# Later steps for the next expert's preparations, and three buffers for activations, in a hybrid decoder layer with 32 experts

## The chip, the cores and the metric

The kernel runs on one core of one Trainium2 chip. The metric is the time on the device, in microseconds (us), as the median of several runs; smaller is better. One further run of the same kernel was taken with the hardware profiler, and its trace is read below.

## The reference, cut to what matters

One layer of a decoder on 1024 tokens of width 1024. First a mixer (dilated attention beside a gated recurrence, one input and one output projection), then a mixture of experts. All in float32. The change lies in the second part:

```
logits = h @ w_router + b_router
top_val, top_idx = top_k(logits, 4)          # 4 of 32 experts for each token
gates = softmax(top_val)
# for each expert e, on the rows that chose it:
hg = rows @ w_gu[e] + b_gu[e]                # 1024 -> 2048
glu, lin = min(hg[:, :1024], 7), clip(hg[:, 1024:], -7, 7)
act = glu * sigmoid(1.702 * glu) * (lin + 1)
y = (act @ w_down[e] + b_down[e]) * gate     # 1024 -> 1024
out[token] += y
x = x + gate_f * RMSNorm_post(out)
```

An expert has 12.6 MB of weights, all 32 have 403 MB, and each is read once.

## The kernel before, in words

**Order of the experts.** After the mixer the experts are sorted by how many rows they got. The sorted place k fixes a capacity `CAPS[k]`: 352, 288, 256, 240, 224, 208, 200, 192, 180, 176, 164, 160, 152, 148, 144, 136 rows for k = 0 to 15, 128 for k = 16 to 29, 64 for k = 30 and 31. Three classes compute them: `Many` (over 128 rows), `Few` (128) and `Half` (64). `ORDER` alternates them: 1, 30, 0, 31, 2, 16, 3, 17, ... 15, 29. So there are 32 rounds of the loop in `moe`, each with a current expert `cur` and a next one `nxt`, and 31 of them prepare a next one.

**Pieces of weights.** A piece is 1 MB of weights: 128 partitions x 4 x 512 float32. It is loaded by the SP queue into `raw` (4 buffers), copied by ScalarE to a rounded high part `wh` (L283, 4 instructions to a piece, 4 buffers), and VectorE writes the rest into `wl` (L284, 4 instructions, 3 buffers). TensorE then multiplies with high and low parts: in `Few` 12 matmuls of 512 columns to a piece (L291, L292, L294), in `Many` 32 (for capacities up to 256: 16 of twice the capacity and 16 of the capacity, L533). An expert has four steps `gu(0)` to `gu(3)` for the first product and two steps `down(0)`, `down(1)` for the second, each of two pieces: 12 pieces.

**Preparations.** `prep()` of the next expert is a generator. Up to its first `yield` it reads the expert's number and its table of rows, issues the indirect DMA that gathers the rows into `xg` (L623, POOL queue; tag `row`, 6 buffers shared with the results `y`), and takes its tiles. The steps behind that turn `xg` on TensorE through PSUM and split it: in `Few` two steps of four transposes (L302, tile `pts`), each with a copy to `xh` on ScalarE (L304) and a subtraction to `xl` on VectorE (L305); in `Many` one step of four transposes for each half of each block of 128 rows (L508, tile `pxb`; L511 ScalarE and L512 VectorE write `xb`), and a last step that turns the bias (L515, tile `pbb`; L517). In `Half` there is one step (L432). The transposes share two PSUM buffers (tag `tp`).

**Activations.** In `Few`, `gu(c)` ends with `swiglu`, whose last instruction writes `act` (L330). A generator `finish` then turns `act` (L302 again, two transposes) and splits it to `ah`, `al`. `Half` has a `finish` too. In `Many` with a capacity of up to 180, or over 256, `down` has a `finish` that turns the results back (L590, tile `pyb`), one step for each block of 128 rows.

**The side queue.** `Side` holds such generators in the order in which they were added, each with a due time. `add` runs the generator to its first `yield` at once. Each piece of weights ends with a call `side()`: it counts one up and takes up to two steps of the generator at the head, if its due time has passed. A generator behind the head is not looked at. With `wait=1` the first steps come at the second call behind `add`. `until(steps)` runs everything down to that generator. The order of tracing is the priority by which a scheduler orders each engine's instructions when the program is built, and each engine runs its own list in order.

One round: `prep()` of the next expert is added, then come `gu(1)`, `gu(2)`, `gu(3)` of the current one, then `until(prep)`, `gu(0)` of the next one, `until(last)`, `down(0)` and `down(1)` of the current one. So the calls of `side()` in a round are: two in each of `gu(1)`, `gu(2)`, `gu(3)`, the next `gu(0)`, `down(0)`, `down(1)`.

Of the kernel before, what the change touches and what calls it, by code (L numbers as in the profile page):

```python
# [121 lines left out]
def moe_biases(g, tc, wp, wk):  # L122
    nc = tc.nc
    bg = wp.tile([128, 2 * FF], F32, name="bgraw", tag="raw")
    nc.gpsimd.memset(bg[64:128], 0.0)
    for s in range(2):
        ld = nc.sync.dma_start(bg[32 * s:32 * s + 32], g.b_gu[0])
        tc.add_manual_dep(ld.ins, g.gathered.name, SYNC, reason="the first rows come first")
    g.bg = wk.tile([128, 2 * FF], F32R, name="bgsplit", tag="bgs", bufs=1)
    nc.scalar.activation(g.bg, bg, AF.Copy)  # L130
    nc.vector.tensor_sub(g.bg[32:64], bg[32:64], g.bg[32:64].bitcast(F32))


def down_biases(g, tc, wk):

    nc = tc.nc
    raw = wk.tile([96, D], F32, name="bdraw", tag="pwl")
    for s in range(3):
        nc.scalar.dma_start(raw[32 * s:32 * s + 32], g.b_down[0])
    g.bd = wk.tile([96, D], F32R, name="bd", tag="wada")  # L140
    nc.vector.tensor_copy(g.bd, raw)
    nc.vector.tensor_sub(g.bd[64:96], raw[64:96], g.bd[64:96].bitcast(F32))
# [525 lines left out]
def moe(g, tc, wp, wk, sm, ps):  # L668
    g.pieces, g.gathered, g.asked = 0, None, None
    todo = [(Many if CAPS[k] > 128 else Few if CAPS[k] > 64 else Half)(g, tc, k, (wp, wk, sm, ps)) for k in ORDER]  # L670
    side = Side()
    cur = todo[0]
    prep = cur.prep()
    side.add(prep)
    side.until(prep)
    side.add(cur.gu(0, side))
    moe_biases(g, tc, wp, wk)
    overflow_lists(g, tc, sm, ps)
    for nxt in todo[1:] + [None]:
        if nxt:  # L680
            prep = nxt.prep()
            side.add(prep)
        side.add(cur.gu(1, side))
        side.add(cur.gu(2, side))
        last = cur.gu(3, side)
        side.add(last)
        if nxt:
            side.until(prep)
            side.add(nxt.gu(0, side))
        side.until(last)  # L690
        side.add(cur.down(0, side))
        last = cur.down(1, side)
        side.add(last)
        if nxt:
            cur = nxt
    side.until(last)
    g.last_y = cur.y[0]
# [80 lines left out]
def ada(g, tc, cst, wk, sm, ps, dram):  # L778
    nc = tc.nc
    cr = wk.tile([8, 128], F32, name="cr", tag="oo")  # L780
    nc.sync.dma_start(cr, g.c.rearrange("o (k p) -> (o k) p", p=128))
    cs = wk.tile([8, 128], F32, name="cs", tag="oo")
    nc.scalar.activation(cs, cr, AF.Sigmoid)
    nc.vector.tensor_mul(cs, cs, cr)
    pt = ps.tile([128, 512], F32, name="pct", tag="tp")
    nc.tensor.transpose(pt[:, :8], cs, g.ident[:8, :8])
    g.cT = cst.tile([128, 8], F32, name="cT")
    nc.vector.tensor_copy(g.cT, pt[:, :8])
    g.onec = cst.tile([128, 1], F32, name="onec")
    nc.vector.memset(g.onec, 1.0)  # L790
    g.mod_d = dram.tile([6, D], F32, name="mod_d")
# [151 lines left out]
def vec_cols(g, tc, cst, wk, sm, ps):  # L943
    nc = tc.nc
    rows = wk.tile([24, 128], F32, name="vrows", tag="oo")
    nc.sync.dma_start(rows[0:8], g.g_pre_mix.rearrange("o (k p) -> (o k) p", p=128))
    nc.sync.dma_start(rows[8:12], g.attn_norm_w.rearrange("o (k p) -> (o k) p", p=128))
    nc.sync.dma_start(rows[12:16], g.hgrn_norm_w.rearrange("o (k p) -> (o k) p", p=128))
    nc.sync.dma_start(rows[16:24], g.hgrn_lb.rearrange("o (k p) -> (o k) p", p=128))
    pt = ps.tile([128, 512], F32, name="pvt", tag="tp")  # L950
    nc.tensor.transpose(pt[:, :24], rows, g.ident[:24, :24])
    v = cst.tile([128, 24], F32, name="vcols")
    nc.vector.tensor_copy(v, pt[:, :24])
    g.gpre, g.anw, g.hnw = v[:, 0:8], v[:, 8:12], v[:, 12:16]
    m = sm.tile([128, 4], F32, name="lbm")
    nc.vector.tensor_max(m, v[:, 16:20], v[:, 20:24])
    e = sm.tile([128, 2, 4], F32, name="lbe")
    for s in range(2):
        nc.vector.tensor_sub(e[:, s], v[:, 16 + 4 * s:20 + 4 * s], m)
    nc.scalar.activation(e, e, AF.Exp)  # L960
    nc.vector.tensor_add(m, e[:, 0], e[:, 1])
    nc.vector.reciprocal(m, m)
    g.lb = cst.tile([128, 4], F32, name="lb")
    g.lb1 = cst.tile([128, 4], F32, name="lb1")
    nc.vector.tensor_mul(g.lb, e[:, 0], m)
    nc.vector.tensor_scalar(g.lb1, g.lb, -1.0, 1.0, op0=OP.mult, op1=OP.add)
# [49 lines left out]
def hgrn_consts(g, tc, cst, wk):  # L1016
    nc = tc.nc
    d = wk.tile([128, 128], F32, name="hdist", tag="vt")
    nc.gpsimd.iota(d, pattern=[[1, 128]], base=0, channel_multiplier=-1, allow_small_or_imprecise_dtypes=True)
    nc.vector.tensor_scalar(d, d, 0.0, None, op0=OP.is_ge)  # L1020
    g.hmask = cst.tile([128, 128], mybir.dt.uint8, name="hmask")
    nc.vector.tensor_copy(g.hmask, d)
    g.at = []
    for i in range(2):
        z = cst.tile([128, 128], F32, name=f"at{i}")
        nc.vector.memset(z, 0.0)
        g.at.append(z)
# [566 lines left out]
@with_exitstack  # L1594
def layer(ctx: ExitStack, tc: tile.TileContext, args):
    g = Ctx()
    for n, a in args.items():
        setattr(g, n, a)
    cst = ctx.enter_context(tc.tile_pool(name="cst", bufs=1))
    g.cst = cst  # L1600
    dram = ctx.enter_context(tc.tile_pool(name="dram", bufs=1, space=DRAM))
    with ExitStack() as mx:
        ps = Pool(mx.enter_context(tc.tile_pool(name="ps", bufs=1, space=PSUM)),
                  {"mm": 2, "s": 2, "tp": 2, "o": 1, "pa": 1})
        big = mx.enter_context(tc.tile_pool(name="big", bufs=1))
        yp = mx.enter_context(tc.tile_pool(name="yp", bufs=1))
        wk = Pool(mx.enter_context(tc.tile_pool(name="wk", bufs=1)),
                  {"pj": 5, "w": 3, "vt": 1, "pt": 2, "wraw": 2, "wada": 1, "acc": 1, "oo": 2, "kk": 1, "pwh": 2, "pwl": 2, "hf": 1})
        cm = mx.enter_context(tc.tile_pool(name="cm", bufs=1))
        sm = mx.enter_context(tc.tile_pool(name="sm", bufs=1))  # L1610
        consts(g, tc, cst, cm, wk)
        ada(g, tc, cm, wk, sm, ps, dram)
        vec_cols(g, tc, cm, wk, sm, ps)
        g.y = [yp.tile([128, T], F32, name=f"y{k}") for k in range(KT)]

        def masks():
            hgrn_consts(g, tc, cm, wk)
            attn_bias(g, tc, cm, wk)

        make_h(g, tc, cm, big, wk, sm, ps, masks)  # L1620
        g.side = chain(*(ada_group(g, tc, q, wk, sm, ps) for q in (1, 2)))
        mixer(g, tc, wk, sm, ps, lambda: moe_setup(g, tc, cm, wk, dram))
        wout_split(g, tc, big, wk)
        bcast_rows(g, tc, wk)
        down_biases(g, tc, wk)
        router_consts(g, tc, cm, wk, sm, ps)
        rows = [mix_out_tile(g, tc, t, wk, sm, ps) for t in range(NT)]
        for t in range(NT + 1):
            if t:
                next(rows[t - 1])  # L1630
            if t < NT:
                next(rows[t])
            if t and t < NT - 1:
                next(rows[t])
            if t:
                next(rows[t - 1])
            if t in (0, NT - 1):
                next(rows[t])
            if 1 < t < NT:
                next(rows[t - 2], None)  # L1640
            if t >= NT - 1:
                next(rows[t - 1], None)
        sort_experts(g, tc, cst, sm, ps)
    ps = Pool(ctx.enter_context(tc.tile_pool(name="ps2", bufs=1, space=PSUM)), {"mm": 3, "tp": 2})
    wp = Pool(ctx.enter_context(tc.tile_pool(name="wp", bufs=1)), {"raw": 4, "wh": 4, "wl": 3})
    wk = Pool(ctx.enter_context(tc.tile_pool(name="wk2", bufs=1)),
              {"row": 6, "xh": 1, "xl": 1, "ah": 1, "al": 1, "xb": 1, "ab": 1, "gl": 2, "sg": 1,
               "gm": 1, "sga": 1, "lc": 1, "act": 1})
    sm = ctx.enter_context(tc.tile_pool(name="sm2", bufs=1))
    moe(g, tc, wp, wk, sm, ps)  # L1650
    final_load(g, tc, wk, sm)
    overflow(g, tc, wp, wk, sm, ps)
    final(g, tc, wp, wk, sm)
# [22 lines left out]
```

## Time and profile before

| what | value |
| --- | --- |
| median of 3 runs | 2327.73 us (2326.22 to 2332.06) |
| the profiled run | 2331.19 us |
| its span, first to last instruction | 2329.6 us |
| TensorE busy with matmuls | 2204.8 us (95%) |
| VectorE, ScalarE, GpSimd busy | 1762.8 us (76%), 1437.5 us (62%), 275.4 us (12%) |
| moved by DMA | 530.24 MB, mean 228 GB/s |
| mean granted TensorE clock | 0.975 |

The mixer takes about the first 710 us, the experts run from there to about 2290 us, and what is left is the last norm and the sum. Times in the rows below are in us from the start of the span, durations of single instructions in ns where marked. "PEclk" is the granted TensorE clock as a share of the full one: 1.00 is 2.4 GHz, 0.50 is 1.2 GHz.

### The profile page before, as it was taken

Reading aid. Unit: us, or ns where it says so; the run is one execution under the profiler, and the core shown is the slowest. Engines: PE = TensorE matmul, PEld = TensorE weight load, DVE = VectorE, ACT = ScalarE, POOL = GpSimd, SP = SyncE. Lnnn points to the kernel's source line nnn. Section 1 sums busy time; section 2 is a strip of 40 time slices with the busy share of each in tenths; the row PEclk is TensorE's granted clock in tenths of the full one; section 3 lists DMA queues with packets and bytes.
Section 4 is the critical chain, followed back from the end, with each engine's and each line's share of the span. In section 5 each row is a group of like instructions: output and inputs, shape, how many; then the busy total and the mean of one; then the engine's idle time right before and its main releaser. Section 6 shows DMA issues by size and latency. Waiting matters only on the chain. (4 is left out here: it accounts for less than half of the span.)

```text
span 2329.6 us, 38808 instructions
## 1 busy us (share of the span) xinstructions
PE 2204.8 (95%) x13342; PEld 1867.8 (80%) x13342; DVE 1762.8 (76%) x3887; ACT 1437.5 (62%) x3092; POOL 275.4 (12%) x239
## 2 busy tenths in 40 slices
PE   6999999998986999999999999999999999999992
PEld 3766667886766999788798888979899899899891
DVE  5466647556776675778797887979889899988985
ACT  6343442324545675767676776767777777777773
POOL 2000000000233020211011111101111111111000
PEclk8999999998997999999999999999999999999996
DMA  6333201113348695979798988989989999999997
GB/s 256 118 100 100 83 19 49 39 46 114 113 151 247 213 284 175 292 221 304 246 310 267 287 285 269 318 262 310 300 287 318 311 306 318 307 314 313 309 314 228
DMA packets 399937, 530.24 MB, mean 228 GB/s; under 512 B 17284, under 2 KB 308412, under 8 KB 398648
## 3 DMA queue, kind: packets, MB, share of 16 engines
q1 hardware_dynamic: 382736, 477.18, 61.6%
q0 software_dynamic: 15664, 45.92, 8.6%
q10 hardware_dynamic: 1336, 4.63, 0.5%
q8 instruction: 106, 1.74, 0.3%
q14 instruction: 95, 0.78, 0.1%
HBM read 487.91 MB, written 39.75 MB: 227 GB/s over the span
## 5 line engine op out<-in xcount | busy, mean ns | idle before, releaser
L284 DVE TENSOR_TENSOR wl<-raw,wh 128x512 fp32r<-128x512 f32 x1536 | 976.3, 686 | 153.1 <-ACT wh L283 60.5
L283 ACT ACTIVATE wh<-raw 128x512 fp32r<-128x512 f32 x1536 | 852.4, 623 | 240.4 <-DMA raw<-in_w_down_dram 61.1
L533 PE MATMUL pgb<-xb,wh 128*128 128x288 f32 (+13 forms) x2304 | 473.1, 333 | 3.2 <-DVE gl L553 2.8
L533 PEld LDWEIGHTS pgb<-xb,wh 128*128 128x128 f32 x2304 | 360.5, 190 | 11.9 <-DVE gl L553 3.5
L533 PE MATMUL pgb<-xb,wl 128*128 128x288 f32 (+15 forms) x2048 | 301.3, 274 | 0.0
L533 PEld LDWEIGHTS pgb<-xb,wl 128*128 128x128 f32 x2048 | 290.6, 190 | 5.3
L632 POOL DMA_INDIRECT yacc<-y,tab x52 | 111.3, 2141 | 1033.2 <-ACT y L373 487.7
L291 PE MATMUL pg<-wh,xh 128*128 128x512 f32 x448 | 180.3, 402 | 0.0
L292 PE MATMUL pg<-wh,xl 128*128 128x512 f32 x448 | 175.2, 391 | 0.0
L533 PE MATMUL pdb<-ab,wh 128*128 128x288 f32 (+7 forms) x768 | 142.5, 314 | 0.0
L551 ACT ACTIVATE gl<-pgb,bcol 128x288 f32<-128x288 f32 (+15 forms) x256 | 94.1, 421 | 75.5 <-PE pgb L533 75.2
L995 PE MATMUL pp<-hh,pwh 128*128 128x512 f32 x448 | 130.6, 411 | 7.5 <-DVE y L1055 4.4
L995 PE MATMUL pp<-hl,pwh 128*128 128x512 f32 x448 | 130.8, 408 | 0.9 <-DVE hl L932 0.9
L995 PE MATMUL pp<-hh,pwl 128*128 128x512 f32 x448 | 129.2, 406 | 0.0
L294 PE MATMUL pg<-wl,xh 128*128 128x512 f32 x448 | 120.1, 390 | 0.0
L533 PEld LDWEIGHTS pdb<-ab,wh 128*128 128x128 f32 x768 | 115.1, 189 | 1.1 <-DVE yt L581 0.2
L995 PEld LDWEIGHTS pp<-hh,pwh 128*128 128x128 f32 x448 | 82.3, 193 | 26.1 <-DVE y L1055 4.8
L294 PEld LDWEIGHTS pg<-wl,xh 128*128 128x128 f32 x448 | 84.1, 188 | 18.0
L291 PEld LDWEIGHTS pg<-wh,xh 128*128 128x128 f32 x448 | 84.2, 188 | 16.8
L995 PEld LDWEIGHTS pp<-hh,pwl 128*128 128x128 f32 x448 | 81.6, 190 | 19.7 <-issue 5.4
L292 PEld LDWEIGHTS pg<-wh,xl 128*128 128x128 f32 x448 | 84.3, 188 | 15.8
L369 PE MATMUL pd<-wh,ab 128*128 128x512 f32 (+5 forms) x384 | 96.8, 394 | 0.0
(447 smaller groups left out, 3416.2 us busy)
## 6 DMA issues: line engine op xcount, KB each, us to landing
raw<-in_w_gu_dram SPq DMA_DIRECT2D x512, 512.0 KB
raw<-in_w_down_dram SPq DMA_DIRECT2D x128, 1024.0 KB
wada<-in_w_ada_dram SPq DMA_DIRECT2D x32, 512.0 KB
wraw<-in_w_in_dram SPq DMA_DIRECT2D x28, 512.0 KB
wada<-in_w_ada_dram SPq DMA_DIRECT2D x8, 1024.0 KB
x<-in_x_dram SPq DMA_DIRECT2D x8, 512.0 KB
oraw<-in_w_out_dram SPq DMA_DIRECT2D x8, 512.0 KB
xo<-in_x_dram SPq DMA_DIRECT2D x8, 512.0 KB
```

Of the source, the lines that this page charges most:

```text
L283: nc.scalar.activation(h, r, AF.Copy)
L284: nc.vector.tensor_sub(lo, r, h.bitcast(F32))
L291: nc.tensor.matmul(out, xh[:, k0 + i, :], wh[:, i, :], start=start and i == 0, stop=False)
L292: nc.tensor.matmul(out, xl[:, k0 + i, :], wh[:, i, :], start=False, stop=False)
L294: nc.tensor.matmul(out, xh[:, k0 + i, :], wl[:, i, :], start=False, stop=stop and i == HK - 1)
L369: nc.tensor.matmul(p[j][:r], m(j, a, s * HK + i), w[:, i, :], start=s + a + i == 0 and w is wh, stop=s == 1 and w is wl and i == HK - 1)
L533: nc.tensor.matmul(o, w, x, start=s == 0 and j == 0, stop=s == 1 and j == len(seq) - 1, skip_group_check=True)
L551: nc.scalar.activation(gl[:, t, h], src, AF.Identity, bias=self.bias[:, j:j + 1])
L632: b.tc.nc.gpsimd.indirect_dma_start(out=b.g.yacc[:, :], out_offset=bass.IndirectOffsetOnAxis(ap=rows, axis=0), in_=y, in_offset=None, comp ...
L995: nc.tensor.matmul(p, a[:, kt, :], b[:, kt, hs], start=n == 0, stop=n == 3 * KT - 1)
```

## The change

A generator of preparations is now added with a wait of two calls, except in the two rounds whose current expert is of class `Half`. The tag `act` gets three buffers where it had one.

```diff
@@ moe
     for nxt in todo[1:] + [None]:
         if nxt:
             prep = nxt.prep()
-            side.add(prep)
+            side.add(prep, 1 if isinstance(cur, Half) else 2)
         side.add(cur.gu(1, side))
         side.add(cur.gu(2, side))
         last = cur.gu(3, side)
@@ layer
     wk = Pool(ctx.enter_context(tc.tile_pool(name="wk2", bufs=1)),
               {"row": 6, "xh": 1, "xl": 1, "ah": 1, "al": 1, "xb": 1, "ab": 1, "gl": 2, "sg": 1,
-               "gm": 1, "sga": 1, "lc": 1, "act": 1})
+               "gm": 1, "sga": 1, "lc": 1, "act": 3})
```

## Rows read from the trace of the kernel before

**Rows 1.** Stretches: us, then busy us of each engine, PEclk, DMA share, GB/s.
```profile
1600.00:1800.00 200.00, 200.00 (x1273) 184.81 (x1271) 177.79 (x344) 153.04 (x318) 29.65 (x21) 1.00 0.95 302
2000.00:2200.00 200.00, 198.60 (x1310) 180.28 (x1309) 179.71 (x357) 154.66 (x326) 30.23 (x22) 1.00 0.96 308
```

**Rows 2.** Waits of TensorE, 710 to 2300 us: total us, times, longest us.
```profile
PE pts L302 <- DMA xg<-hrows,tab: 5.0, 1, 5.0
PE pbb L515 <- DVE xb L512: 4.0, 5, 1.3
PE pts L302 <- DVE act L330: 4.0, 1, 4.0
PE pgb L533 <- DVE gl L553: 2.8, 5, 1.1
...
PE pts L302 <- DVE xb L512: 0.7, 3, 0.3
```

**Rows 3.** Timeline of TensorE around 988 us: start, length, what, idle before.
```profile
988.17 1.97 PE L302 MATMUL pts<-ident,xg 128*128 128x128 f32 x8 [4.95 <-DMA xg<-hrows,tab]
...
992.40 1.09 PE L533 MATMUL pgb<-xb,wh 128*128 128x512 f32 x4
...
993.81 1.09 PE L533 MATMUL pgb<-xb,wh 128*128 128x512 f32 x4
```

**Rows 4.** The stretch with the lower clock, columns as in the first group.
```profile
985.50:992.20 6.70, 4.03 (x15) 3.65 (x16) 2.44 (x5) 2.62 (x5) 1.43 (x1) 0.50 1.03 294
```

**Rows 5.** Timeline of GpSimd, the gather for expert 16.
```profile
973.74 8.50 POOL L623 DMA_INDIRECT xg<-hrows,tab  x1 [4.68 <-DMA tab<-table]
```

**Rows 6.** Timeline of VectorE in the same stretch.
```profile
972.83 8.52 DVE L284 TENSOR_TENSOR wl<-raw,wh 128x512 fp32r<-128x512 f32 x14
...
983.36 2.49 DVE L284 TENSOR_TENSOR wl<-raw,wh 128x512 fp32r<-128x512 f32 x4
```

**Rows 7.** Tile xg: all its gathers (ns min/median/max), and issue to landing.
```profile
L623 POOL DMA_INDIRECT xg<-hrows,tab x50: 920/1129/8501, 713.8 to 2193.2; - x50
...
DMA to landing us min/median/max: 5.8/6.9/8.7
```

**Rows 8.** Timeline of TensorE, second transposes and bias for expert 5.
```profile
1255.00 0.88 PE L508 MATMUL pxb<-ident,xg 128*128 128x128 f32 x8
...
1259.50 0.23 PE L515 MATMUL pbb<-ident,br 16*128 16x16 f32 x1 [0.60 <-DVE xb L512]
```

**Rows 9.** Timeline of ScalarE beside them.
```profile
1257.09 1.15 ACT L283 ACTIVATE wh<-raw 128x512 fp32r<-128x512 f32 x2 [0.80 <-DMA raw<-in_w_gu_dram]
1258.14 0.90 ACT L511 ACTIVATE xb<-pxb 128x512 fp32r<-128x512 f32 x2
```

**Rows 10.** Timeline of TensorE, the same work for expert 9.
```profile
1638.41 1.04 PE L590 MATMUL pyb<-ident,yt 128*128 128x128 f32 x8
...
1646.06 0.97 PE L508 MATMUL pxb<-ident,xg 128*128 128x128 f32 x8
...
1649.89 0.23 PE L515 MATMUL pbb<-ident,br 16*128 16x16 f32 x1
```

**Rows 11.** Timeline of ScalarE beside them.
```profile
1647.25 0.79 ACT L511 ACTIVATE xb<-pxb 128x512 fp32r<-128x512 f32 x2
```

**Rows 12.** Timelines of TensorE, ScalarE and VectorE, turning the rows of expert 17.
```profile
1094.05 1.03 PE L302 MATMUL pts<-ident,xg 128*128 128x128 f32 x8
...
1094.95 1.08 ACT L304 ACTIVATE xh<-pts 128x512 fp32r<-128x512 f32 x2
...
1095.75 1.28 DVE L305 TENSOR_TENSOR xl<-pts,xh 128x512 fp32r<-128x512 f32 x2
```

**Rows 13.** VectorE by line, 1600 to 2200 us: busy us, mean ns, idle before.
```profile
L330 DVE SCALAR_TENSOR_TENSOR act<-lc,gm 128x256 f32<-128x256 f32 x28 | 11.8, 422 | 1.9 <-PE pts L302 1.9
```

**Rows 14.** Waits of the DMA queue of the weights, 710 to 2300 us.
```profile
SPq L310 <- DVE wl L284: 566.2, 239, 8.0
SPq L316 <- DVE wl L284: 499.2, 124, 9.2
```

## The prediction

> **What bounds the kernel now.** I read the table of stretches first, then TensorE's waits, then the timelines of the engines at the longest of them. From 1600 to 1800 us TensorE is busy in all 200.00 us at a clock of 1.00, and from 2000 to 2200 in 198.60, with VectorE next at 178 to 180 and the DMA engines at a share of 0.95 [rows 1]. So with the experts an edit is worth what it takes from TensorE's waits, and no more. The DMA share looks like a second bound, but the queue that loads the weights spends 566.2 + 499.2 us of this part waiting until VectorE frees a buffer [rows 14]: the loads are held back, not late on the whole.
>
> TensorE's waits in this part are few [rows 2]. The reader is to see three that touch the change: one of 5.0 us for the gathered rows of a `Few` expert, five that make 4.0 us ahead of the transposed bias of a `Many` expert, and three that make 0.7 us ahead of the transposes right behind it. Two others matter less: 2.8 us in five for a PSUM buffer that VectorE empties, and 4.0 us for the last expert's activations.
>
> **The change part by part.** Which rounds move? By `Side`, steps added with `wait=2` come at the third call instead of the second, that is behind the first piece of `gu(2)` instead of behind `gu(1)`. Two of the 31 rounds have a `Half` as current expert and keep 1. In seven (current experts 22 to 28) the queue's head is the down `finish` of the `Many` before; it takes its two steps at the second call, and the preparations start at the third one already. That leaves 22: two preparations of `Half`, 14 of `Few`, six of `Many` (experts 3 to 8). What comes before the first `yield` (register loads, table, gather, bias load) runs in `add` and is not moved, so the POOL and SP queues keep their order. Moved are transposes on TensorE, their copies on ScalarE and subtractions on VectorE. No instruction is added.
>
> *The wait for the gather.* It is in the first preparation of a `Few`, for expert 16. TensorE stopped 4.95 us and went on at 988.17 [rows 3], so it came there at 983.22. The gather had been at work on GpSimd from 973.74 to 982.24 [rows 5] and landed 5.9 us later, near the fastest of all gathers (5.8) [rows 7]. A piece of this expert takes 5.64 us: eight matmuls go by from 992.40 to 993.81, 1.41 us [rows 3], and a piece has 32. With the transposes one piece later TensorE gets there at 983.22 + 5.64 = 988.86, 0.7 us behind the landing. The wait goes. With it goes what it cost afterwards: during the stop the granted clock fell to 0.50 (1.2 GHz) and stood there from 985.5 to 992.2, and TensorE worked 4.03 us of that [rows 4], 2.0 us more than at full clock. Together 7.0 us. What comes next there is the first tile of the second piece, which waits for nothing that the trace shows. Bounds: if the gather lands as slowly as the slowest (8.7 us), at 990.9, 2.1 us of waiting stay and the gain is 4.9; the upper end is 7.0. I take 7.0. The other 13 `Few` preparations show no such wait and gain nothing here.
>
> Why did that gather take 8.50 us on GpSimd, where the median is 1.129 us [rows 5, 7]? Beside it VectorE ran 14 subtractions without a break, 972.83 to 981.35, and the gather was through 0.9 us after the last [rows 6].
>
> The Trainium skill, "SBUF — State Buffer", section "SBUF: two separate sides", says that VectorE and GpSimd share one pair of ports as an exclusive lock, and that a DMA issued by GpSimd can't write its descriptors while VectorE holds it. By that rule the landing hangs on where VectorE's run breaks off, not on the gather's place in its queue; this trace agrees, with the 0.9 us above. As the run lies ahead of the moved steps, the rule leaves the sum as it is, but it makes a rival, below.
>
> *The waits at the bias.* The bias goes into the PSUM buffer of the third `pxb`, so it waits for VectorE's `xb` of that one. For expert 5, TensorE turned the second pair at 1255.00 to 1255.88, but ScalarE's copies began at 1258.14, since weight splits stood ahead of them in its list, and these waited for their load (0.80 us) [rows 8, 9]. The seven rounds that already run in the new order are a natural test: for expert 9 the second pair began at 1646.06, ScalarE's copies came at 1647.25, and the bias at 1649.89 waited for nothing [rows 10, 11]; none of the seven has such a wait, all five lie before 1600 us. But they differ in one thing: 16 transposes back (`pyb`, 1.04 us for eight [rows 10]) stretch the round and give the weights time. Bounds: all 4.0 + 0.7 = 4.7 us go; or, as the steps come nearer to the pieces that wait for their loads, each of six rounds waits the longest seen, 1.3 us, which is 7.8 - 4.7 = 3.1 us worse. The seven rounds are nearest. I take two thirds of the gain, 3.0 us.
>
> *The moved copies of `Few`.* Two copies (1.08 us) and two subtractions (1.28 us) [rows 12] now come inside `gu(2)` and no longer beside the emptying of `gu(1)`'s PSUM. Cover: ScalarE and VectorE run some pieces ahead of TensorE. Bounds: the five PSUM waits (2.8 us [rows 2]) go, or the 1.28 us come on the path in each of 14 rounds, 17.9 us. I take 0: VectorE has some 20 us idle in 200 [rows 1], and the work is the same.
>
> *Three buffers.* With the moved order the activation of `gu(1)` is turned behind the writing of that of `gu(2)`. In the seven rounds that did so with one buffer, VectorE waited 1.9 us in all [rows 13], and TensorE not at all. So the buffers gain 0, and they avoid that wait in six rounds more. The rows `xg` stay one piece longer, up to 5.64 us here; gathers run tens of us ahead of their transposes but for expert 16, so that costs 0.
>
> Sum: 7.0 + 3.0 = 10.0 us. Of the profiled run: 2331.19 - 10.0 = 2321.2; what lies outside the span (1.6 us) stays. The median of the runs shown is 3.46 us below the profiled one, so I forecast 2327.73 - 10.0 = 2317.7 us.
>
> **The rivals.**
> 1. Only the gather's wait goes, and ScalarE's list holds the second pair back as before. For it: the load that held it back is still there. Against: the seven rounds. 2327.7 - 7.0 = 2320.7.
> 2. The gather slips. Two `Half` preparations upstream move as well, and VectorE's run before 981 us may come without its break, on through the four subtractions that end at 985.85 [rows 6]. Then the gather is through at 986.7 and lands at 992.6, 3.7 us behind TensorE, which costs that and up to 2.0 for the clock: of 10.0 some 4.3 stay, or 1.3 without the bias. About 2325. Against: the margin is small, but nothing moved lies between 972 and 983. The page named above is what makes it thinkable.
> 3. The order on TensorE hardly changes, since a scheduler has the last word. Against: each block of the trace follows the traced order, but for a few by the first experts. 2327.7.
> 4. Slower: the moved copies stand in VectorE's list ahead of the splits that TensorE needs next, and each of the 14 `Few` preparations delays it by 1.28 us: 2327.7 - 10.0 + 17.9 = 2335.6. For it: VectorE is busy 0.89 of the time, and TensorE did wait for its emptying five times. It decides from 10.0 / 14 = 0.7 us a round. Against: with the same copies beside the emptying itself these waits make only 2.8 us in all.
>
> **How the numbers follow.** Chances: forecast 0.50, rival 1 0.20, rival 2 0.14, rival 3 0.05, rival 4 0.11. A measurement here can tell about 0.3%, 7.0 us, from no change, so the lines are 2320.7 and 2334.7. Of the forecast 0.44 is faster and 0.06 (gather or bias worth less) within; rival 1 lies on the line, 0.10 each; rivals 2 and 3 are within, 0.19; rival 4 is slower by 0.10 and within by 0.01. Faster 0.54, same 0.36, slower 0.10. Range: the best case is 7.0 + 4.7 + 2.8 = 14.5 us, 2313.2; upwards it has to hold rivals 2 and 3 and the noise of a median, 2328.5. Outside are rival 4 and some 0.06 below.
>
> **What would show it.** Right: in TensorE's waits the row for `xg` is gone or under 1 us, the clock is 1.00 around 988, the transposes of expert 16 stand 32 matmuls later, and the bias waits sum to under 2 us. Wrong: a wait for `xg` of 2 us or more, wherever it stands; bias waits of 4 us or more; or new waits for `wl` or PSUM that sum to over 5 us from 1000 to 2275 us.

## The result, and the profile after

Over 10 runs each, the changed kernel takes 2339.43 us (median; 2334.67 to 2347.94) and the kernel before 2326.36 us (2321.1 to 2332.06). The ratio is 1.0063 with a 95% interval of 1.0049 to 1.0077: slower by some 13 us. The forecast was 2317.7 us, a range of 2313.0 to 2328.5, and a chance of 0.10 for slower.

The two profiled runs lie closer together, 2331.19 and 2335.55 us, since the first was one of the slower runs of its kernel and the second one of the faster. The page of the changed kernel, its span and TensorE's busy time:

```profile
span 2333.9 us, 38806 instructions
...
PE 2204.9 (94%) x13342; PEld 1868.0 (80%) x13342; DVE 1761.3 (75%) x3887; ACT 1437.7 (62%) x3092; POOL 260.8 (11%) x239
```

TensorE's busy time is the same to 0.1 us (2204.8 before), so what this profile loses against the first shows as waiting. TensorE's waits in the part with the experts, columns as in [rows 2]:

```profile
PE pgb L533 <- DVE gl L553: 7.0, 6, 2.0
PE pxb L508 <- DVE xb L512: 6.0, 6, 1.3
PE pts L302 <- DVE act L330: 4.5, 2, 2.9
PE pbb L515 <- DVE xb L512: 1.8, 5, 0.5
PE pdb L533 <- DVE yt L581: 1.0, 1, 1.0
...
PE pts L302 <- DVE xb L512: 0.7, 3, 0.3
```

Against [rows 2] the row for `xg` is gone (5.0 us) and the bias waits fell from 4.0 to 1.8. But there is a new row of 6.0 us in six, ahead of the second pair of transposes `pxb`, and the waits for a PSUM buffer rose from 2.8 to 7.0.

**The gather.** The gather on GpSimd, and the transposes of expert 16, which answer to [rows 5] and [rows 3]:

```profile
968.33 1.21 POOL L623 DMA_INDIRECT xg<-hrows,tab  x1 [4.59 <-DMA tab<-table]
```

```profile
985.85 1.04 PE L302 MATMUL pts<-ident,xg 128*128 128x128 f32 x8
```

Nothing waits there, and the clock stayed at 1.00. But this gather took 1.21 us on GpSimd, not 8.50, so it would not have been late in its old place either.

**The second pair.** TensorE and ScalarE in the round of expert 16, which prepares expert 3:

```profile
1039.67 0.98 PE L508 MATMUL pxb<-ident,xg 128*128 128x128 f32 x8
...
1044.82 1.13 PE L508 MATMUL pxb<-ident,xg 128*128 128x128 f32 x8 [1.15 <-DVE xb L512]
...
1049.02 0.23 PE L515 MATMUL pbb<-ident,br 16*128 16x16 f32 x1 [0.31 <-DVE xb L512]
```

```profile
1040.99 0.63 ACT L283 ACTIVATE wh<-raw 128x512 fp32r<-128x512 f32 x1 [2.51 <-DMA raw<-in_w_gu_dram]
1042.41 1.15 ACT L283 ACTIVATE wh<-raw 128x512 fp32r<-128x512 f32 x2 [0.78 <-DMA raw<-in_w_gu_dram]
1043.46 1.01 ACT L511 ACTIVATE xb<-pxb 128x512 fp32r<-128x512 f32 x2
```

The first pair was turned by 1040.65, but ScalarE's copies of it came at 1043.46. Three splits stood ahead of them in its list, and ScalarE sat idle for 2.51 and 0.78 us until their weights had landed. The second pair needs the first one's PSUM buffers, so TensorE stood. In the kernel before, the same three splits stood behind these copies and ahead of the second pair's, as [rows 8, 9] show it for expert 5, and it was the bias that waited.

**The PSUM waits.** Around 2139 us, in the round that prepares expert 28, TensorE, ScalarE and VectorE:

```profile
2130.33 1.05 PE L302 MATMUL pts<-ident,xg 128*128 128x128 f32 x8
...
2138.95 0.79 PE L533 MATMUL pgb<-xb,wh 128*128 128x288 f32 x4 [1.78 <-DVE gl L553]
```

```profile
2133.85 1.67 ACT L283 ACTIVATE wh<-raw 128x512 fp32r<-128x512 f32 x3 [2.04 <-DMA raw<-in_w_gu_dram]
2135.43 1.07 ACT L304 ACTIVATE xh<-pts 128x512 fp32r<-128x512 f32 x2
2136.39 0.63 ACT L283 ACTIVATE wh<-raw 128x512 fp32r<-128x512 f32 x1
2136.91 1.20 ACT L551 ACTIVATE gl<-pgb,bcol 128x144 f32<-128x144 f32 x4
```

```profile
2136.04 1.29 DVE L305 TENSOR_TENSOR xl<-pts,xh 128x512 fp32r<-128x512 f32 x2 [2.53 <-ACT xh L304]
2137.25 1.28 DVE L284 TENSOR_TENSOR wl<-raw,wh 128x512 fp32r<-128x512 f32 x2
2138.45 0.45 DVE L553 TENSOR_TENSOR gl<-gl,pgb 128x288 f32<-128x288 f32 x1
```

The transposes were done at 2131.4. Their copies stood behind three splits that waited 2.04 us for a load, and ahead of the emptying of PSUM (`gl`) in ScalarE's list; in VectorE's list the two subtractions held up the emptying as well. TensorE got its buffer at 2138.95, 1.78 us late. Not all of this is new: in the kernel before, TensorE waited at the same place as well.

```profile
2138.92 0.79 PE L533 MATMUL pgb<-xb,wh 128*128 128x288 f32 x4 [1.02 <-DVE gl L553]
```

By these two profiles 0.76 us of this wait are new; over all rounds the row grew from 2.8 to 7.0 us. Behind the longest wait of the row, 1.99 us at 2230, the granted clock stayed at 1.00; behind this one it fell to 0.50 for 3.4 us, within this stretch:

```profile
2140.00:2144.00 4.00, 4.00 (x23) 4.00 (x21) 3.46 (x10) 1.96 (x5) 2.11 (x3) 0.57 0.93 322
```

### The profile page after: what moved, and what is told of

The parts are those of the page before. It is cut to its first block, busy times and chain, and to the rows that moved or that the text cites. A ratio compares the mean times of both kernels' runs of the same rounds, so it can differ in the third digit from the quotient of the medians.

```text
span 2333.9 us, 38806 instructions
## 1 busy us (share of the span) xinstructions
PE 2204.9 (94%) x13342; PEld 1868.0 (80%) x13342; DVE 1761.3 (75%) x3887; ACT 1437.7 (62%) x3092; POOL 260.8 (11%) x239
```

## The experiments

The first theory after the result: the change is three edits in one, the gather's wait is a gain, and the six preparations of `Many` and the 13 other ones of `Few` each lose more than that. The rival: all moved steps are harmless or good, and the gain is given back elsewhere.

**One preparation alone**, that of expert 16:

```
-            side.add(prep)
+            side.add(prep, 2 if cur.k == 2 else 1)
```

> The due time is moved for one preparation alone, that of expert 16, the first Few; act keeps one buffer. Theory (the gather's wait is a gain, and the other moved preparations lose more than that): the wait of 5.0 us for xg goes and the clock stays at 1.00 around 983 to 992, all else as before: 7 us faster than before, about 2319. Rival (the gain is given back further on, since the loads lose the head start that the stop gave them): within 3 us of before.

Measured: 2320.71 us against 2326.83, ratio 0.9971 (0.9960 to 0.9983). The theory holds. In this profile the gather was slow, and yet nothing waited:

```profile
969.24 11.15 POOL L623 DMA_INDIRECT xg<-hrows,tab  x1 [4.66 <-DMA tab<-table]
```

```profile
987.16 1.04 PE L302 MATMUL pts<-ident,xg 128*128 128x128 f32 x8
```

**The 13 other preparations of `Few` alone:**

```
-            side.add(prep)
+            side.add(prep, 2 if isinstance(cur, Many) and cur.k > 2 else 1)
```

> The due time is moved for the 13 other preparations of class Few alone; act keeps one buffer. Theory (the copies to xh and xl now stand ahead of the emptying of PSUM in the lists of ScalarE and VectorE): the wait for xg of 5.0 us stays, TensorE's waits for PSUM (pgb behind gl) rise from 2.8 to about 7 us, all of it in the last seven of these rounds, where a piece takes least time: 5 to 8 us slower, about 2333. Rival (these rounds are as good as before, and the whole loss is with the Many preparations): same within 2 us.

Measured: 2334.26 us against 2326.83, ratio 1.0037 (1.0022 to 1.0051). TensorE's waits from 1600 us on:

```profile
PE pgb L533 <- DVE gl L553: 6.9, 7, 1.9
```

As the theory said, and all seven lie behind 1860 us. The steps `gu(1)` to `gu(3)` of `Many` from 1050 us on, from the first matmul of each `gu(1)` to the first of the `Few` behind it, take 367.9 us in all, against 358.4 with the three buffers alone. That is more than the waits grew, since the clock stood at 0.50 for 10.2 us behind one of them; TensorE worked through nearly all of that, which makes some 5 us by estimate.

**The six preparations of `Many` alone:**

```
-            side.add(prep)
+            side.add(prep, 2 if type(cur) is Few else 1)
...
-               "gm": 1, "sga": 1, "lc": 1, "act": 1})
+               "gm": 1, "sga": 1, "lc": 1, "act": 3})
```

> The due time is moved for the six preparations of class Many in rounds of class Few alone, with three buffers for act. Theory (ScalarE's list has the first pair of copies behind splits that wait for their load, and the second pair of transposes waits for the first pair's buffer): a wait of 0.7 to 1.5 us ahead of the second pair (pxb) in each of the six rounds, 6 us, and 1.8 us at the bias in place of 4.0: 4 to 6 us slower, about 2332. Rival (the step as I predicted it): 3 us faster, no wait at pxb.

Measured: 2335.82 us against 2326.83, ratio 1.0044 (1.0027 to 1.0061). TensorE's waits from 1030 to 1600 us:

```profile
PE pxb L508 <- DVE xb L512: 6.9, 6, 1.8
PE pbb L515 <- DVE xb L512: 1.9, 5, 0.6
PE pts L302 <- DVE xb L512: 0.7, 3, 0.3
```

The six rounds, from the first matmul of `gu(1)` to the first of the next expert's `gu(0)`, take 129.4 us against 121.8 with the buffers alone. Of these 7.6 us the waits make 5.8 (9.5 against 3.7), and TensorE's busy time, which grew from 117.9 to 119.5 us, nearly all of the rest. The loss in time, 9.0 us, is above the 4 to 6 that I expected.

**The three buffers alone:**

```
-               "gm": 1, "sga": 1, "lc": 1, "act": 1})
+               "gm": 1, "sga": 1, "lc": 1, "act": 3})
```

> Only the three buffers for act. TensorE's, ScalarE's and the queues' lists are those of before; in seven rounds VectorE writes act one instruction earlier. Theory: its wait of 1.9 us goes, and the time is the same within 2 us, 2326. Rival (the 2 KB more move the tiles behind them in memory, and that costs in every run): 5 us slower or more, with the same waits.

Measured: 2327.82 us against 2326.83, ratio 1.0003 (0.9989 to 1.0017): nothing. Its profiled run took 2320.31 us, without a wait for `xg`, though the transposes stood in their old place. It is the better partner for the changed kernel's profile: spans of 2318.7 and 2333.9 us, both without that wait, differ by 15.2, of which the six rounds of `Few` make 6.7 and the late steps of `Many` 6.6.

**Why the second pair waits.** The splits of the next expert's first piece are ordered behind the first pair's copies, in the six rounds and in the seven later ones that prepare a `Many`, all else as with the six `Many` preparations. TensorE's list stays the same, and so do the queues'; VectorE's subtractions follow ScalarE's new order.

```
# split(..., after=()), for each high part:
hi = nc.scalar.activation(h, r, AF.Copy).ins
for x in after:
    tc.add_manual_dep(hi, x.name, NOSYNC, reason="rows first")
# piece(), for (c, s) == (0, 0) of a Many with k > 2: after = the first two xb copies of prep()
```

> As the kernel with only the Many preparations moved, but the splits of the next expert's first piece are ordered behind the first pair's two copies (xb) in ScalarE's list. TensorE's list is the same instruction by instruction. Theory (the pair's copies stood behind three splits that wait for their load): the waits ahead of the second pair of transposes (6.9 us in six) fall below 1 us, those at the bias stay at 2 to 3 us, and the time is 4 to 7 us below that kernel, about 2330. Rival (the waits come from VectorE's backlog or from the transposes' place itself): the waits stay at 5 us or more, 2336.

Measured: 2327.23 us against 2324.85, ratio 1.0013 (0.9996 to 1.0030). ScalarE in the round that prepares expert 3, and TensorE's waits from 1030 to 1600 us:

```profile
1049.17 1.03 ACT L511 ACTIVATE xb<-pxb 128x512 fp32r<-128x512 f32 x2 [1.82 <-PE pxb L508]
1050.09 0.63 ACT L283 ACTIVATE wh<-raw 128x512 fp32r<-128x512 f32 x1
1051.16 2.23 ACT L283 ACTIVATE wh<-raw 128x512 fp32r<-128x512 f32 x4 [0.44 <-DMA raw<-in_w_gu_dram]
```

```profile
PE pbb L515 <- DVE xb L512: 1.9, 3, 1.0
PE pd L369 <- DVE al L305: 0.6, 1, 0.6
PE pts L302 <- DVE xb L512: 0.5, 2, 0.3
```

The row of 6.9 us is gone, the six rounds take 120.7 us in place of 129.4, and of the 9.0 us some 2.4 are left, which the interval does not tell from none. So it was the copies' place in ScalarE's list, behind splits that wait for their load, and nothing about the transposes' place on TensorE.

**The kernel before, once more:**

> The kernel before once more, one execution. Theory (the gather for expert 16 loses a race with VectorE's run of 14 subtractions in some executions and not in others): either the gather takes 8 us or more on GpSimd and TensorE waits some 5 us for xg, or it takes under 2 us and nothing waits; the span differs by about 7 us between the two. Rival (the wait is the same in every execution): 8.5 us again and 5 us of waiting.

Measured: 2330.4 us in the one run. The gather was slow again, and TensorE waited:

```profile
970.49 9.86 POOL L623 DMA_INDIRECT xg<-hrows,tab  x1 [4.87 <-DMA tab<-table]
```

```profile
986.46 1.97 PE L302 MATMUL pts<-ident,xg 128*128 128x128 f32 x8 [4.71 <-DMA xg<-hrows,tab]
```

Alone it doesn't tell the theory from the rival; with the other profiles it does. In seven the transposes of expert 16 are in their old place. In four of these the gather took 8.50 to 11.37 us on GpSimd and TensorE waited 4.7 to 5.2; in three it took 1.02 to 1.44 and nothing waited. In the six with the new place it was slow four times (8.24 to 11.15) and nothing ever waited.

**Why the PSUM waits.** The 13 `Few` preparations by three calls:

```
-            side.add(prep)
+            side.add(prep, 3 if isinstance(cur, Many) and cur.k > 2 else 1)
```

> As the kernel with only the 13 other Few preparations moved, but by three calls: the transposes come behind the second piece of gu(2), where they stand to the emptying of gu(2) as they stood before to that of gu(1). Theory (what costs is the place of the copies ahead of an emptying of PSUM): the waits for PSUM fall back to 1 to 3 us and the time to that of before, 2327. Rival (a later place is worse in itself, since VectorE has less room there): waits of 7 us or more, 2334 or more.

Measured: 2326.02 us against 2324.85, ratio 1.0013 (0.9994 to 1.0033). ScalarE in the round that prepares expert 28, and the waits from 1600 us on:

```profile
2136.95 1.17 ACT L551 ACTIVATE gl<-pgb,bcol 128x144 f32<-128x144 f32 x4
2138.00 1.10 ACT L304 ACTIVATE xh<-pts 128x512 fp32r<-128x512 f32 x2
```

```profile
PE pdb L533 <- DVE yt L581: 2.3, 2, 1.6
PE pgb L533 <- DVE gl L553: 2.1, 3, 1.1
```

The copies stand behind the emptying, and the waits for PSUM are back at 2.1 us. A later place is not worse in itself: two calls cost 7 us, three cost nothing that can be told. Whether it is ScalarE's list or VectorE's that costs the 7 us, these runs do not separate. A wait of 2.3 us at `down` is new, in a single profile.

**The Many preparations earlier.** Expert 16 by two calls, and the steps of `Many` in rounds of `Few` one piece earlier than before:

```
-            side.add(prep)
+            side.add(prep, 2 if cur.k == 2 else 0 if type(cur) is Few else 1)
```

> The preparation of expert 16 by two calls, those of Many in rounds of class Few by none (one piece earlier than before), all others by one; act keeps one buffer. Theory (the later in a Few expert, the longer the copies stand behind splits that wait for their loads): no wait at pxb, those at the bias fall from 4 us to under 1, so 3 to 5 us below the kernel with the preparation of expert 16 alone: about 2317, faster than both kernels. Rival (TensorE then waits elsewhere in the same rounds): same as that kernel, 2321.

Measured: 2318.54 us against 2324.85, ratio 0.9977 (0.9964 to 0.9990): faster than both kernels, but no better than expert 16 alone (0.9971). The mechanism came as expected: from 1030 to 1600 us TensorE waits for nothing, and the six rounds take 117.8 us against 121.2 there. The time does not show it; but 3.4 us are 0.0015 of the whole, and the two intervals overlap (0.9964 to 0.9990 and 0.9960 to 0.9983).

Three single runs asked why, and whether the changed kernel's profile was typical.

> The kernel with the Many preparations one piece earlier, a second execution with a profile. Theory (what it gains before 1600 us it gives back later, since TensorE then runs closer to the loads): no wait at bias or pxb before 1600 us, and waits for PSUM of 4 us or more behind it, against 2 to 3 in the kernel with the preparation of expert 16 alone, whose lists from 1600 us on are the same. Rival (the waits for PSUM differ from execution to execution by as much): under 3 us here, or over 4 there.

> The kernel with only the preparation of expert 16 moved, a second execution with a profile. Theory: waits for PSUM of 2 to 3 us from 1600 us on, bias waits of 2 to 4 us before it, no wait for xg whatever the gather takes on GpSimd. Rival (they differ from execution to execution): PSUM waits over 4 us.

> The changed kernel, a second execution with a profile. Theory: again six waits ahead of the second pair of transposes that sum to 5 to 8 us, PSUM waits of 6 us or more, and no wait for xg. Rival (the first profile was an outlier): one of the two sums under half of that.

Measured: 2321.53, 2318.18 and 2344.29 us. With the early `Many` the six rounds again take 117.7 us, and the waits for PSUM were 4.5 us the first time and now 3.1; with expert 16 alone 2.1 and 2.2:

```profile
PE pgb L533 <- DVE gl L553: 3.1, 4, 1.1
```

```profile
PE pgb L533 <- DVE gl L553: 2.2, 3, 1.1
```

The expectation of 4 us or more failed. The waits lean the way the theory says, by 1 to 2 us. The late steps of `Many`, measured as above, lean that way too: 360.6 and 359.3 us with the early `Many` against 357.8 and 358.0 with expert 16 alone, so that 1 to 3 of the 3.4 us are given back there. Whether the rest is lost at all stays open. The changed kernel's second profile confirms the first:

```profile
PE pxb L508 <- DVE xb L512: 7.7, 6, 1.9
PE pgb L533 <- DVE gl L553: 6.4, 6, 1.9
PE pbb L515 <- DVE xb L512: 1.0, 3, 0.3
```

Here the gather took 8.88 us, again without a wait for `xg`. The span is 8.7 us longer than in the first profile: the first `pxb` comes 4.1 us later, and the clock stood at 0.50 for 3.4 us at 1155 and for 10.2 us at 2234, each behind a wait.

## Why the prediction was wrong

**Which steps move**: right but for one. On TensorE 21 of the 22 preparations stand one piece later; the transposes of the first `Half` (expert 30) stand behind the first 112 matmuls of expert 1 in both kernels.

**The wait for the gather, 7.0 us**: right. With that step alone the kernel is 6.1 us faster. The steps around it (`gu(1)` to `gu(3)` of expert 2) take 41.4 to 41.9 us with the wait and 34.3 without, 7.1 to 7.6. What I did not see in one execution is that some executions are spared. If the gather is slow as often as in the 13 profiles, in eight, the mean gain is some 4.5 us by estimate; the interval of the run, 4.0 to 9.3 us, holds that and 7.0.

**The waits at the bias, "I take two thirds of the gain, 3.0 us"**: this step failed, and in its sign. In its place stands a loss of 9.0 us. I took the seven rounds that already ran in the new order as a test. Their order is indeed the new one, on TensorE and on ScalarE: in all 13 preparations of `Many` behind 1000 us in the changed kernel, the first pair's copies stand behind the first three splits of the next expert's first piece, with five more splits ahead of the second pair's (VectorE's lists differ by one or two splits). What differs is the load. This is ScalarE in the round of [rows 10, 11], in the kernel before:

```profile
1640.72 2.33 ACT L283 ACTIVATE wh<-raw 128x512 fp32r<-128x512 f32 x4
1642.96 0.80 ACT L511 ACTIVATE xb<-pxb 128x512 fp32r<-128x512 f32 x2
```

The weights of these splits had landed, ScalarE waited at most 0.1 us ahead of them in each of the seven rounds, and the copies began while the transposes were still under way (1642.04 to 1643.02). In the six rounds of the changed kernel it sat idle ahead of the same splits for 2.1 to 2.6 us and then for some 0.8 us more. I had named what sets the seven apart (the transposes back "stretch the round and give the weights time") and gave it no price; whether it is these transposes that do it, no run tests. I had also named the load as the cause of the bias waits, and rival 1 says that it "is still there", but at no loss. The bound beside it ("as the steps come nearer to the pieces that wait for their loads") had the direction, but 3.1 us as its end. By waits alone it is 9.5 us (6.9 + 1.9 + 0.7) in place of 4.7. And there was less to gain than I read: the seven profiles with these steps in their old place show 2.4 to 4.0 us at the bias, and the one that I had shows the most.

**The moved copies of `Few`, "I take 0"**: this step failed too; it cost 7.4 us. This is near rival 4, but it was the emptying of PSUM that came late and not the splits, and the price is smaller than its 17.9: the late rounds alone pay, where a piece takes least time. My reason, that VectorE has 20 us idle in 200, is a mean, and it says nothing of what stands ahead of what. I gave that rival 0.11.

**Three buffers, 0**: right within the measurement.

The parts sum to -6.1 + 9.0 + 7.4 = 10.3 us, with the buffers inside the 9.0, against 13.1 measured for the whole. The two preparations of `Half` are in none of the parts; what is missing, 2.8 us, is less than the intervals of the parts leave open. With the gather's term right and the two others 12.0 and 7.4 us off, the forecast came out at the wrong side.

The signs that I had set for being right all came true in the changed kernel's first profile: no wait for `xg`, the clock at 1.00 around 988, the transposes of expert 16 32 matmuls later, 1.8 us at the bias. The first two were luck there, since its gather was a fast one. Of the signs for being wrong only the new waits for PSUM showed, and they were enough: 6.0 us at `pxb`, and 7.0 in place of 2.8 at `pgb`.

## What to carry to other kernels

When a step is traced later, look where its instructions land in the list of every engine that takes part: a copy behind a split that waits for a load inherits that wait, and a copy ahead of an emptying of PSUM passes its own on. A stretch that already runs in the new order is a test only if what its instructions wait for comes as early there: here ScalarE's list was the same, and the loads were not. Split a change with one good place and many others by place: here one preparation of 22 held all the gain that the runs show.

## What the runs showed of the hardware

The same gather, behind the same instructions, took 1.02 to 1.44 us on GpSimd in five of 13 profiles and 8.24 to 11.37 in eight. In each of the eight it was done 0.9 us after the last of VectorE's 14 subtractions. The start does not decide alone: one that began 2.0 us ahead of the run was held for 11.37 us, one that began 2.5 ahead took 1.02, and one that began 1.3 us inside the run took 1.44. Nor is the run a start: in all 13 profiles VectorE has no break of 0.3 us in the 8 us ahead of it, so each of these gathers began beside a busy VectorE. And it is not the gather alone: in the five profiles where it came through, the scatter behind it on GpSimd began 0.5 to 3.1 us inside the run; four times it took 1.55 to 2.01 us, once 9.06 us, done 1.35 us after the run's end.

The Trainium skill, "SBUF — State Buffer", section "SBUF: two separate sides", says that the pair of ports which the two engines share is an exclusive lock: the one that starts first has it for its whole instruction, and the other blocks. For a VectorE instruction with two inputs in SBUF, as these subtractions have, the section says so only against a GpSimd instruction that reads SBUF; that the gather is one (its row numbers lie in the tile `tab`) is how I read the program, and no run shows it. The eight agree with a block until VectorE's last instruction ends. By that rule alone the gather that began inside the run and came through is not what one would expect, nor are the ones that began ahead of the run and were held, unless it is the instructions before the run that held them; no run here shows what lets a gather pass.
